# The beginning of a decoder layer: table load, first transfers, single k-tiles and the order of the first chunk

## The chip, the cores and the metric

The kernel runs on one core of a Trainium2 chip. The metric is the time of the program on the device in microseconds (us), the median of several executions; lower is better. A profiled execution gives the trace from which the rows below are read. Engines are named as the profile names them: PE (TensorE, matrix products), PEld (its weight loads), ACT (ScalarE), DVE (VectorE), POOL (GpSimd), SP (SyncE, which here only issues transfers). ACTq and SPq are the sequencers' transfer issues.

## What is computed

One layer of a hybrid decoder trunk on 256 tokens of width 2048. For the change only its beginning matters: the normalised memory `mem` times its key and value weights, before the input projection of `x`.

```python
def rms_norm(x, g):
    xf = x.astype(jnp.float32)
    y = xf * lax.rsqrt(jnp.mean(xf * xf, axis=-1, keepdims=True) + NORM_EPS)
    return (y * g.astype(jnp.float32)).astype(x.dtype)

def hybrid_layer(x, mem, ...):
    h = rms_norm(x, g_mix)
    proj = h @ w_in
    ...                                   # pooling, sparse attention
    mem_h = rms_norm(mem, g_mem)
    kv_m = mem_h @ w_mem_kv               # 256 x 2048 times 2048 x 1024
    k_m = rms_norm(kv_m[..., :XATTN_W].reshape(B, M, XATTN_HEADS, HEAD_DIM), xk_norm_g)
    v_m = kv_m[..., XATTN_W:].reshape(B, M, XATTN_HEADS, HEAD_DIM)
    ...                                   # cross attention, gates, output projection
    x = x + hierarchical_moe(rms_norm(x, g_ffn), ...)
    return x
```

## The kernel before

Products are made with split operands: each f32 operand is written as a high part (rounded, on ACT) and a low part (the rest, on DVE), and a product is three matmuls, high times high, high times low and low times high. `split_evac` (line 123) does that for weights: `wh` is a copy on ACT (line 124), `wl` a subtraction on DVE (line 125). `gain_split` (line 190) does it for the transposed activations, one k-tile of 128 x 256 at a time, with the norm's gain (a column of the constants `cs`) folded in: the high part on ACT (line 195), the low part on DVE (line 196).

The memory comes in four quads `memq[0..3]` of four k-tiles (128 x 4 x 256, 512 KB each), the weights of one chunk of 512 columns in four tiles `rawt` of four k-tiles (1 MB each, four buffers). `feeder` (line 229) loads `rawt` tile by tile on SP's queue (`load`, line 198) and, behind each load, what is listed under `after_load`: the next quad of the memory for the first chunk, quads of `x` for the second. Each tile gives two pairs of k-tiles, `wh` and `wl`, in three buffers each. `fetch(n)` draws from the feeder until `n` pairs are ready ahead.

`chunk` (line 259) runs over eight pairs of k-tiles: it fetches up to three pairs ahead, makes the 12 matmuls of a pair (line 274: two token tiles, two k-tiles, three products), then calls `pump`, which advances the background work by one step. During the first chunk, called km, the background is `mem_steps`: for quads 1, 2 and 3 the squares of the quad (`rm.square`, lines 169 and 172 on ACT, the sum with `tensor_add` on POOL, line 173) and its `gain_split`, then an empty step, then `rm.done` (line 175): matmuls that sum the squares (lines 179 and 184), the copy `row` (line 180) and the chain for 1/sqrt (`rsqrt`, lines 147 to 157, 14 operations of 128 x 2 on DVE). The result `rmr` scales the products when they are copied out of PSUM (`km_evac`, line 353). The second chunk, vm, has the same operand and, in the background, the same work on `x` for `hT`, the operand of the third.

The order of the instructions on an engine is set by a scheduler that goes by a timeline of its own. `keep_in_program_order` ties an instruction behind the one that was traced before it on its engine. `pin` (line 110) does so as long as the list `inorder` isn't empty; `load` and `warm` always do. Before the change the list is emptied ahead of the first chunk, behind the first two pairs (line 359).

At the start, 12 matmuls on a zeroed tile `z` run on PE (`warm`, line 301).

Of the kernel before, what the change touches and what calls it, by code (L numbers as in the profile page):

```python
# [15 lines left out]
AF = mybir.ActivationFunctionType  # L16
# [28 lines left out]
C_GMEM = 420  # L45
# [8 lines left out]
def layer_kernel(tc, x, xT, memT, pos, cst, band, gains, bgate, wmem, wxq, widx, wkqvp, wpg, wgb, wo, wr, we, out):  # L54
    nc = tc.nc
    V = nc.vector
    A = nc.scalar
# [50 lines left out]
    inorder = [True]  # L108

    def pin(i):  # L110
        if inorder:
            tc.keep_in_program_order(i)
# [10 lines left out]
    def split_evac(ps, hi, lo):  # L123
        pin(A.activation(hi, ps, AF.Copy))  # L124
        pin(V.tensor_sub(lo, ps, hi))  # L125
# [10 lines left out]
    ones32 = cp.tile([P, 32], F32, name="ones32")  # L136
    V.memset(ones32, 1.0)
    cs = cp.tile([P, C_N], F32, name="cs")
    nc.scalar.dma_start(cs, cst)
    big = cp.tile([P, NT, D], F32, tag="big", name="xin")  # L140
    
    xin = big.rearrange("p t d -> p (t d)").rearrange("p (k s) -> p k s", s=S)
# [16 lines left out]
    class RowRstd:  # L159
# [6 lines left out]
        def square(self, q, src):  # L166
            if q == 0:
                self.acc = scr.tile([P, 4, S], F32, tag="sqa", name="sqa", bufs=1)
                A.activation(self.acc, src, AF.Square)
            else:  # L170
                sq = scr.tile([P, 4, S], F32, tag="sq", name="sqT", bufs=1)
                A.activation(sq, src, AF.Square)
                nc.gpsimd.tensor_add(self.acc, self.acc, sq)

        def done(self):
# [14 lines left out]
    def gain_split(src, gc, dst, q, ks=slice(0, 4)):  # L190

        for k in range(ks.start, ks.stop):
            g = cs[:, gc + 4 * q + k : gc + 4 * q + k + 1]
            hi, lo = dst.q[q][:, 0, k], dst.q[q][:, 1, k]
            pin(A.activation(hi, src[:, k], AF.Copy, scale=g))
            pin(V.scalar_tensor_tensor(lo, src[:, k], g, hi, op0=ALU.mult, op1=ALU.subtract))

    def load(dst, src):
        tc.keep_in_program_order(nc.sync.dma_start(dst, src))
# [3 lines left out]
    def pump(n=1):  # L203
        for _ in range(n):
            while bg:
                try:
                    next(bg[0])
                    break
                except StopIteration:
                    bg.popleft()  # L210

    def drain():
        while bg:
            pump()
# [14 lines left out]
    def feeder():  # L229

        for ci, (src, n) in enumerate(plan):
            for i in range(4):
                rt = raw.tile([P, 4, n], F32, tag="raw", name="rawt")
                if ci == 0 and i == 0:
                    load(rt[:, 0:2], src[:, 0:2, :])
                    load(memq[0][:, 2:4], memT[0][:, 2:4])
                    load(rt[:, 2:4], src[:, 2:4, :])
                else:
                    load(rt, src[:, 4 * i : 4 * i + 4, :])
                for f in after_load.get((ci, i), ()):  # L240
                    f()
                for j in range(2):
                    s = rt[:, 2 * j : 2 * j + 2, :]
                    wh = spl.tile([P, 2, n], F32R, tag="wh", name="wh")
                    wl = spl.tile([P, 2, n], F32R, tag="wl", name="wl")
                    split_evac(s, wh, wl)
                    yield wh, wl

    feed = feeder()
    fed = deque()  # L250

    def fetch(n):
        while len(fed) < n:
            w = next(feed, None)
            if w is None:
                return
            fed.append(w)
# [45 lines left out]
    z = scr.tile([P, 512], BF16, tag="zero", name="zero", bufs=1)  # L303
# [5 lines left out]
    mT = Quads(lambda i: mtp.tile([P, 2, 4, S], F32R, name="memT%d" % i))  # L309
# [4 lines left out]
    def c4(name):  # L314
        return crp.tile([P, 4, S], F32, tag="c4", name=name, bufs=4)
# [11 lines left out]
        return done  # L327

    memq = [c4("memq") for _ in range(4)]
    load(memq[0][:, 0:2], memT[0][:, 0:2])  # L330

    def at(key, fn, *args):
        after_load.setdefault(key, []).append(lambda: fn(*args))
# [6 lines left out]
    def mem_steps():  # L340
        for q in range(1, 4):
            rm.square(q, memq[q])
            gain_split(memq[q], C_GMEM, mT, q)
            yield
        yield
        yield from rm.done()
# [5 lines left out]
            km.append(tok(c4("km")))  # L352
        A.activation(km[0][:, t], ac, AF.Copy, scale=rm.r[:, t : t + 1])

    gain_split(memq[0], C_GMEM, mT, 0, slice(0, 2))
    fetch(1)
    gain_split(memq[0], C_GMEM, mT, 0, slice(2, 4))
    fetch(2)
    inorder.clear()
    rm.square(0, memq[0])  # L360
    bg.append(mem_steps())
    chunk(512, [(KD, mT, km_evac)], name="km")
    drain()
    km = km[0]

# [170 lines left out]
    bias = [ap.tile([P, (t + 1) * P], F32, name="bias%d" % t) for t in range(NT)]  # L536
# [785 lines left out]
```

## Time and profile before

| | before |
|---|---|
| median of 3 runs | 1180.93 us (1178.69 to 1185.09) |
| the profiled execution | 1179.43 us |
| its span, first to last instruction | 1177.6 us |
| PE busy | 1146.5 us, 97% of the span |
| DVE busy | 576.6 us, 49% |
| ACT busy | 424.4 us, 36% |
| POOL busy | 30.3 us, 3% |
| granted clock of PE, mean | 0.992 |

The profiled execution is 1.8 us longer than its span; that is what lies around the first and the last instruction. A row of a timeline has the start in us, the time in us, the engine, the line, the operation, what it writes and reads, how many instructions are merged in it, and in brackets how long the engine was idle ahead of it and what ended that. A merged row's time runs from the start of its first instruction to the end of its last. Ends of matmuls are modelled, so the distance of their starts says more than their length.

### The profile page before, as it was taken

What the parts mean: (1) busy time and instruction counts of PE and PEld (TensorE: products, weight loads), DVE (VectorE), ACT (ScalarE), POOL (GpSimd) and SP (SyncE); (2) the same over time, 40 slices, a digit from 0 to 9 for tenths busy, and PEclk for the clock granted to TensorE, in tenths of its full rate; (3) what the DMA queues carried; (4) which work ended last, traced back from release to release, by engine and by line L of the source; (5) the groups of instructions that cost most, each with busy time, mean ns of one, the idle gap of its engine ahead of it and who ended that gap; (6) DMA issues with size and microseconds to landing.
All of it is one profiled execution on the core that took longest, in us unless ns stands there. A gap on an engine that the chain in (4) does not pass through costs nothing.

```text
span 1177.6 us, 14726 instructions
## 1 busy us (share of the span) xinstructions
PE 1146.5 (97%) x5863; PEld 790.0 (67%) x5863; DVE 576.6 (49%) x946; ACT 424.4 (36%) x664; POOL 30.3 (3%) x33
## 2 busy tenths in 40 slices
PE   8999999999999999999999999999999999999986
PEld 5788887888878888888888776454534544363423
DVE  7877468956546456456555445231413332151202
ACT  7665574445644444444444443111101201020100
POOL 4200000000000000000000000000000000000000
PEclk9999999999999999999999999989999999999998
DMA  9546554555645555555698759989999999999995
GB/s 382 203 129 229 184 178 146 178 186 179 225 157 200 208 193 205 201 194 208 219 346 359 281 212 339 423 340 426 425 427 426 425 427 427 425 425 427 425 427 218
DMA packets 50190, 342.45 MB, mean 291 GB/s; under 512 B 5696, under 2 KB 6336, under 8 KB 10432
## 3 DMA queue, kind: packets, MB, share of 16 engines
q1 hardware_dynamic: 46800, 331.93, 72.6%
q0 software_dynamic: 1728, 7.15, 1.7%
q10 hardware_dynamic: 1584, 2.34, 0.6%
q8 instruction: 48, 0.79, 0.3%
q14 instruction: 30, 0.25, 0.1%
HBM read 337.20 MB, written 4.19 MB: 290 GB/s over the span
## 4 chain that ended last, share of the span: by engine, by line


## 5 line engine op out<-in xcount | busy, mean ns | idle before, releaser
L274 PE MATMUL acc<-wh,hT 128*128 128x512 f32 (+1 forms) x1280 | 396.0, 388 | 0.0
L125 DVE TENSOR_TENSOR wl<-rawt,wh 128x1024 fp32r<-128x1024 f32 (+1 forms) x240 | 289.8, 1210 | 210.0 <-ACT wh L124 209.0
L124 ACT ACTIVATE wh<-rawt 128x1024 fp32r<-128x1024 f32 (+1 forms) x240 | 250.8, 1048 | 297.8 <-PE acc L274 290.9
L274 PEld LDWEIGHTS acc<-wh,hT 128*128 128x128 f32 x1280 | 238.3, 188 | 46.6 <-issue 0.3
L274 PE MATMUL acc<-wl,hT 128*128 128x512 f32 (+1 forms) x640 | 249.2, 390 | 0.0
L274 PEld LDWEIGHTS acc<-wl,hT 128*128 128x128 f32 x640 | 120.2, 188 | 24.0 <-DVE isc L585 0.3
L833 PE MATMUL gu<-we,xg 128*64 128x512 f32 x464 | 103.8, 595 | 1.8 <-DMA we<-in_we_dram 1.8
L274 PE MATMUL acc<-wh,mgT 128*128 128x512 f32 x256 | 81.7, 397 | 0.0
L833 PEld LDWEIGHTS gu<-we,xg 128*64 128x64 f32 x464 | 32.2, 137 | 64.8 <-issue 55.3
L958 ACT ACTIVATE xs<-x 128x256 fp32r<-128x256 f32 x61 | 24.8, 415 | 97.7 <-PE sm L833 86.9
L1169 DVE TENSOR_TENSOR x<-x,sm 128x512 f32<-128x512 f32 (+1 forms) x66 | 41.3, 668 | 38.0 <-PE sm L833 38.0
L1159 ACT ACTIVATE ob<-dn 128x512 fp32r<-128x512 f32 (+1 forms) x33 | 19.3, 585 | 104.1 <-PE dn L833 97.9
L274 PEld LDWEIGHTS acc<-wh,mgT 128*128 128x128 f32 x256 | 47.9, 188 | 11.4 <-issue 0.4
L1160 DVE TENSOR_TENSOR ob<-dn,ob 128x512 fp32r<-128x512 f32 (+1 forms) x33 | 22.3, 675 | 66.0 <-ACT ob L1159 65.9
L274 PE MATMUL acc<-wl,mgT 128*128 128x512 f32 x128 | 51.2, 400 | 0.0
L1146 DVE SCALAR_TENSOR_TENSOR sgm<-sgm,fac,gu 128x512 f32<-128x512 f32 x8 | 6.0, 748 | 90.8 <-PE gu L833 90.8
L1138 ACT ACTIVATE sgm<-gu,fac 128x512 f32<-128x512 f32 x8 | 5.5, 687 | 115.9 <-PE gu L833 69.2
L833 PE MATMUL dn<-we,aT 128*64 128x256 f32 x384 | 45.6, 384 | 1.4 <-ACT aT L1153 1.4
L833 PE MATMUL gu<-wm,xg 128*64 128x512 f32 x184 | 43.5, 594 | 1.3 <-DMA wm<-in_we_dram 1.3
L833 PE MATMUL gu<-wh,xg 128*64 128x512 f32 x200 | 44.7, 595 | 0.0
L274 PE MATMUL acc<-wh,memT 128*128 128x512 f32 x128 | 42.4, 408 | 1.3 <-ACT wh L124 1.3
L833 PE MATMUL gu<-wr,xg 128*64 128x512 f32 x176 | 41.7, 594 | 0.5 <-DMA wr<-in_we_dram 0.5
(338 smaller groups left out, 1196.4 us busy)
## 6 DMA issues: line engine op xcount, KB each, us to landing
we<-in_we_dram SPq DMA_DIRECT2D x82, 1024.0 KB, 19.4
rawt<-in_wgb_dram SPq DMA_DIRECT2D x64, 1024.0 KB, 4.8
wh<-in_we_dram SPq DMA_DIRECT2D x37, 1024.0 KB, 19.2
wr<-in_we_dram SPq DMA_DIRECT2D x36, 1024.0 KB, 19.5
wm<-in_we_dram SPq DMA_DIRECT2D x36, 1024.0 KB, 19.5
rawt<-in_wkqvp_dram SPq DMA_DIRECT2D x24, 1024.0 KB, 4.9
rawt<-in_wo_dram SPq DMA_DIRECT2D x16, 1024.0 KB, 4.9
rawt<-in_wmem_dram SPq DMA_DIRECT2D x7, 1024.0 KB, 8.3
```

What stands on the lines that cost most here:

```text
L124: pin(A.activation(hi, ps, AF.Copy))
L125: pin(V.tensor_sub(lo, ps, hi))
L274: m = mm(o, a[:, c], w[:, kk], start=st, stop=sp)
L833: i = mm(*a, **k)
L958: pin(A.activation(xs[:, 0], x2[:, :, c], AF.Copy))
L1138: A.activation(sg, ag, AF.Sigmoid, scale=r2s)
L1146: V.scalar_tensor_tensor(sg, sg, c1s, au, op0=ALU.mult, op1=ALU.mult)
L1159: A.activation(ob[:, 0], ad, AF.Copy)
L1160: V.tensor_sub(ob[:, 1], ad, ob[:, 0])
L1169: V.tensor_add(ys, ys, ps)
```

## The change

The constants `cs` and the first quad of the memory are issued on ACT's queue, the quad in pieces (k-tile 0, then `cs`, k-tile 1, k-tiles 2 and 3), while SP's queue begins with the weights, now in pieces of one, one and two k-tiles. A one-element copy on ACT stands behind these issues, ahead of the first gain. The first two pairs are split k-tile by k-tile: gain of a k-tile, then its weights, from inside the feeder. `rm.square` is pinned too, and the list `inorder` is emptied behind the first chunk, not ahead of it.

```diff
     cs = cp.tile([P, C_N], F32, name="cs")
-    nc.scalar.dma_start(cs, cst)
...
             if q == 0:
                 self.acc = scr.tile([P, 4, S], F32, tag="sqa", name="sqa", bufs=1)
-                A.activation(self.acc, src, AF.Square)
+                pin(A.activation(self.acc, src, AF.Square))
             else:
                 sq = scr.tile([P, 4, S], F32, tag="sq", name="sqT", bufs=1)
-                A.activation(sq, src, AF.Square)
+                pin(A.activation(sq, src, AF.Square))
                 nc.gpsimd.tensor_add(self.acc, self.acc, sq)
...
                 if ci == 0 and i == 0:
-                    load(rt[:, 0:2], src[:, 0:2, :])
-                    load(memq[0][:, 2:4], memT[0][:, 2:4])
+                    load(rt[:, 0:1], src[:, 0:1, :])
+                    load(rt[:, 1:2], src[:, 1:2, :])
                     load(rt[:, 2:4], src[:, 2:4, :])
...
-                    split_evac(s, wh, wl)
+                    if ci == i == 0:
+
+                        for kk in range(2):
+                            k = 2 * j + kk
+                            gain_split(memq[0], C_GMEM, mT, 0, slice(k, k + 1))
+                            split_evac(s[:, kk], wh[:, kk], wl[:, kk])
+                    else:
+                        split_evac(s, wh, wl)
                     yield wh, wl
...
     memq = [c4("memq") for _ in range(4)]
-    load(memq[0][:, 0:2], memT[0][:, 0:2])
+
+    def load2(dst, src):
+        tc.keep_in_program_order(nc.scalar.dma_start(dst, src))
+
+    load2(memq[0][:, 0:1], memT[0][:, 0:1])
+    load2(cs, cst)
+    load2(memq[0][:, 1:2], memT[0][:, 1:2])
+    load2(memq[0][:, 2:4], memT[0][:, 2:4])
+
+    tc.keep_in_program_order(A.activation(ones32[:, 0:1], z[:, 0:1], AF.Copy, bias=1.0))
...
-    gain_split(memq[0], C_GMEM, mT, 0, slice(0, 2))
-    fetch(1)
-    gain_split(memq[0], C_GMEM, mT, 0, slice(2, 4))
     fetch(2)
-    inorder.clear()
     rm.square(0, memq[0])
     bg.append(mem_steps())
     chunk(512, [(KD, mT, km_evac)], name="km")
+    inorder.clear()
     drain()
```

## Rows read from the trace of the kernel before

**Rows 1.** Windows: start:end, length, busy time and instructions per engine, PEclk, DMA.

```profile
0.00:61.00 61.00, 55.37 (x229) 39.64 (x230) 49.36 (x76) 42.79 (x70) 20.43 (x14) 0.97 0.73 284
61.00:200.00 139.00, 139.00 (x665) 115.70 (x664) 96.50 (x220) 82.59 (x176) 1.10 (x2) 1.00 0.53 177
...
630.00:720.00 90.00, 89.64 (x442) 70.88 (x440) 41.26 (x44) 36.47 (x47) 0.50 (x2) 1.00 0.75 281
...
800.00:900.00 100.00, 98.38 (x598) 48.93 (x596) 30.80 (x60) 14.18 (x29) 0.00 (x0) 1.00 1.01 426
```

**Rows 2.** Timeline of PE, 0 to 61 us.

```profile
1.23 5.13 PE L301 MATMUL warm<-zero 128*128 128x512 bf16 x12 [1.23 <-DVE zero L304]
7.68 0.73 PE L274 MATMUL acc<-wh,memT 128*128 128x512 f32 x2 [1.32 <-ACT wh L124]
...
15.48 0.86 PE L274 MATMUL acc<-wh,memT 128*128 128x512 f32 x3
...
18.70 0.86 PE L274 MATMUL acc<-wh,memT 128*128 128x512 f32 x3
...
27.51 0.40 PE L274 MATMUL acc<-wh,memT 128*128 128x512 f32 x1
...
34.32 0.63 PE L274 MATMUL acc<-wh,memT 128*128 128x512 f32 x2
...
49.90 0.64 PE L179 MATMUL ssT<-sqa,ones 128*32 128x256 f32 x8 [0.97 <-POOL sqa L173]
...
52.50 0.50 PE L274 MATMUL acc<-wl,memT 128*128 128x512 f32 x1 [1.30 <-DVE wl L125]
...
60.96 0.62 PE L274 MATMUL acc<-wh,hT 128*128 128x512 f32 x2
```

**Rows 3.** Timeline of DVE, 17 to 34 us.

```profile
17.50 3.81 DVE L196 SCALAR_TENSOR_TENSOR memT<-memq,cs,memT 128x256 fp32r<-128x256 f32 x4
21.23 2.35 DVE L125 TENSOR_TENSOR wl<-rawt,wh 128x1024 fp32r<-128x1024 f32 x2
...
27.25 2.34 DVE L125 TENSOR_TENSOR wl<-rawt,wh 128x1024 fp32r<-128x1024 f32 x2
...
30.98 1.66 DVE L196 SCALAR_TENSOR_TENSOR hT<-xin,cs,hT 128x256 fp32r<-128x256 f32 x4
...
33.95 0.16 DVE L187 TENSOR_SCALAR rmv<-ssv 128x2 f32<-128x2 f32 x1
```

**Rows 4.** Timeline of POOL, the first two sums of squares.

```profile
11.35 2.49 POOL L173 TENSOR_TENSOR sqa<-sqa,sqT 128x1024 f32<-128x1024 f32 x1 [10.04 <-ACT sqT L172]
15.79 4.05 POOL L173 TENSOR_TENSOR sqa<-sqa,sqT 128x1024 f32<-128x1024 f32 x1 [1.95 <-ACT sqT L172]
```

**Rows 5.** Timeline of ACT, 0 to 46 us.

```profile
0.73 0.41 ACTq L139 DMA_DIRECT2D cs<-in_cst_dram  x1
4.48 1.28 ACT L195 ACT_TABLE_LOAD   x1 [4.48 <-DMA memq<-in_memT_dram]
...
10.23 1.04 ACT L172 ACTIVATE sqT<-memq 128x1024 f32<-128x1024 f32 x1
11.17 1.69 ACT L195 ACTIVATE memT<-memq,cs 128x256 fp32r<-128x256 f32 x4
12.77 1.99 ACT L124 ACTIVATE wh<-rawt 128x1024 fp32r<-128x1024 f32 x2
...
45.16 1.27 ACT L353 ACTIVATE km<-acc,rmr 128x512 f32<-128x512 f32 x2 [3.07 <-DVE rmr L156]
```

**Rows 6.** Transfers: engine, count, size, us from issue to landing; issues at 0.7, 0.7, 3.2.

```profile
cs<-in_cst_dram ACTq DMA_DIRECT2D x1, 239.0 KB, 3.8
memq<-in_memT_dram SPq DMA_DIRECT2D x1, 256.0 KB, 3.7
...
rawt<-in_wmem_dram SPq DMA_DIRECT2D x1, 1024.0 KB, 8.3
```

**Rows 7.** Windows of 1 us: columns as in the first group.

```profile
10.00:11.00 1.00, 1.00 (x4) 0.81 (x3) 0.65 (x1) 1.00 (x2) 0.00 (x0) 0.50 0.97 406
```

**Rows 8.** Timeline of SP: the issue of the second weight tile.

```profile
3.24 0.44 SPq L199 DMA_DIRECT2D rawt<-in_wmem_dram  x1
```

## The prediction

> **What bounds the kernel now.** I read the windows of the whole span first, then the timelines of PE, ACT, DVE and POOL over the first 61 us. The windows [rows 1] say where a change at the beginning can be felt at all: in 0 to 61 us PE works 55.37 us, and in the next window it works 139.00 of 139.00; the five windows from 61 to 720 us hold 658.6 of 659 us. So nothing after 61 us absorbs or adds anything until 720 us: whatever the start is worth must be there when the matmuls on hT begin, at 60.96 in the execution before [rows 2], and from there it goes to the end one for one. Behind 720 us the expert weights fill the DMA engines (426 GB/s, share 1.01); their transfers start as PE frees buffers, so I let that stretch move along. The question is thus one number: when do the hT matmuls begin?
>
> The PE timeline [rows 2] gives the milestones. The 12 warm-up matmuls end at 6.36, the first real one begins at 7.68. I count in pairs of k-tiles, 12 matmuls each (2 token tiles x 2 k-tiles x 3 products). Pair 1 ends with the first matmul of the row at 15.48, pair 2 with the first of the row at 18.70, pair 5 with the row at 27.51, pair 7 (the last of chunk km) with the first of the row at 34.32: about 15.7, 18.9, 27.9 and 34.5. A matmul takes 0.233 from start to start at full clock (0.86 for three, less the 0.40 of the last, over two steps), so a pair costs 2.8.
>
> The DVE timeline [rows 3] shows the other bound. From 17.50 it works without a pause: four low parts of gain_split take 3.81, two wl 2.35, and so on. At 30.98 four low parts take only 1.66. The difference is POOL: its second add runs from 15.79 to 19.84 [rows 4], the low parts that begin at 17.50 end 1.5 behind that, and so I read that a low part is held until a running add ends. A wl subtraction is not held, but an add that meets two of them takes 4.05 in place of 2.49.
>
> **The table load.** Before, ACT loads its table from 4.48 to 5.76 [rows 5], because the load stands behind the wait for cs (issued 0.73, landed after 3.8: 4.53) and for memq (3.7) [rows 6]. After, ACT issues four transfers at 0.41 each (0.73 to about 2.4), then loads (1.28), done near 3.7, under the flight of the data. That removes 1.28 from ACT's start, if the data is there. It is not: cs is now second on its queue behind 128 KB, with the SP queue's weights beside it. Before, cs and memq, 495 KB, were there at 4.5; after, 128 + 239 KB on ACT's queue and as much of the weights are 734 KB, and at the 406 GB/s of a full window [rows 7] 239 KB more are 0.59: 5.1. If the 1 KB pieces of the single k-tile get a third of the engines instead of half, it is 862 KB, 5.4. If ACT's queue is served first, 4.4. I take 5.2: the first gain begins 0.55 earlier, not 1.28.
>
> The DMA engines are full in that row (share 0.97). The Trainium skill, "DMA: Bandwidth & Descriptors", section "Issuing engines are not separate DMA queues", says that transfers issued from several engines run on the same 16 DMA engines and interleave, and that spreading them saves issue time only. That speaks against this edit, and the full windows here agree: by it the edit is worth at most an issue time, where two independent paths would bring cs at 4.4 and the weights no later.
>
> **Single k-tiles.** A copy of 256 columns costs ACT 0.42 (four in 1.69), of 1024 columns 1.0 (two in 1.99) [rows 5]; 512 columns, which the trace lacks, lie between, in proportion 0.6. On DVE 0.42 and 1.17 give 0.67. So gain and wh of k-tile 0 end near 6.2 and the first matmul could begin there; the warm-ups hold PE to 6.36. PE starts 1.3 earlier than before. Cutting adds 2 x 0.6 - 1.0 = 0.2 to ACT and as much to DVE per pair; both wait for data there, so I put it at nothing; without that cover it is 0.4 for the two pairs. Pair 0 then ends near 10 and pair 1 near 12.9, against 15.7: a lead of 2.8, part of which is the half-clock stretch of before (granted clock 0.50 in 10:11 [rows 7]). The SP queue loses the two memq issues, which moves its later issues up by 0.9; as the engines are full, the landing of the next weights does not follow: the bytes ahead of it are the same.
>
> **Order kept.** This is the edit that decides. With inorder cleared only behind the chunk, every split, gain and square of km stays on ACT and DVE in the order of the code. That order is: wh of pair 2, square 1, gains q1, wh of pair 3, square 2, gains q2, wh 4, square 3, gains q3, wh 5, 6, 7. Before, the scheduler had square 1 (10.23) and gains q1 (11.17) ahead of wh 2 and 3 (12.77) [rows 5], likewise q2 ahead of 4 and 5, q3 ahead of 6 and 7. Two prices follow.
>
> First, wh 2 needs the second weight tile, which lands at 3.24 + 8.3 = 11.5 [rows 6, 8]. ACT, done with the first quad near 10.3, waits; behind it square 1 is queued, then the gains of q1. So wh 2 runs 11.5 to 12.5, square 1 ends at 13.5, the add runs to about 16.1 (before: 13.84), and the low parts of q1 end one by one from 16.5, in place of 14.3. Pair 2 can't use them sooner and ends near 19.0, before 18.9. The lead of 2.8 is used up here.
>
> Second, the low parts of q3 now stand ahead of wl 5, and all low parts are held by their adds. On DVE: low parts of q1 to 17.7, wl 3 to 18.9; add 2 begins behind those low parts and meets wl 3, 2.49 + 1.2, so to 21.3; low parts of q2 (1.66, the first with the add's end) to 22.9, wl 4 to 24.0; add 3 begins behind the low parts and meets wl 4, to 26.4; low parts of q3 to 28.1, wl 5 to 29.2, wl 6 30.4, wl 7 31.5. Before, wl 5 ended at 21.23 + 2.35 = 23.6 and wl 7 near 29.6 (27.25 + 2.34) [rows 3]. Pair 3 ends at 21.9; pair 4 between 25.0 and 26.7, as PE does the products without wl early or late; pair 5 between 30.1 and 31.8 (before 27.9), pair 7 between 36.8 and 38. Chunk km ends 2.3 to 3.5 later; I take 3.0.
>
> **Chunk vm.** Before, it loses 0.97 to POOL and 1.30 to wl [rows 2], as the chain for rmr, begun at 33.95 [rows 3], ends at 45.1 between other work, and the copy of km at 45.16, with 3.07 of waiting ACT [rows 5], holds the squares and gains behind it. After, wl 7 is queued behind the copy of row, and wl 8 behind the whole chain (each pinned instruction follows the one traced before it), so the chain runs undisturbed (15 operations of 0.16: 2.5) and km's copy is not late; the 2.27 may come back wholly or not at all, I take half, 1.1. The price: vm's first pair waits for the chain, from nothing (sums of row placed early among PE's matmuls) to about 5 (behind pair 7); I take 0.6. Sum: +3.0 - 1.1 + 0.6 = **+2.5** on the profiled execution's 1179.43, which lies 1.5 under the median; on the median 1180.93 it is **1183.4**. Its own range is +1 to +5: 1181.9 to 1185.9.
>
> **The rivals.**
> *The early start survives.* PE begins 1.3 earlier and does not stop, so the half-clock stretch goes: about eight matmuls at 0.43 in place of 0.233 cost 1.6. Together -2.9: 1178.0. The Trainium skill, "TensorE: Matmul & The Clock Gate", Part 1, has the clock halved behind idleness and full behind steady work; the row at 0.50 stands behind the gaps up to 7.68, which agrees. It needs gains of q1 that aren't late; for it speaks that the walk above rests on an order which I read from the code, against it the landing at 11.5. Chance 0.20.
> *The two ends cancel.* DVE's work to 61 us is nearly the same in both kernels, 49.36 [rows 1], and as it begins past 6 some 5 us of pauses are the reserve; if vm gives back all 2.27 and the chain hides, the hT matmuls begin within 0.7 of 60.96: 1181. This is also the case in which the change does not do what it says, as PE's end of vm is DVE's. Chance 0.20.
> *The chain stands in the way.* wl 8 waits on DVE behind the chain, the chain waits for the sums of row on PE, and these stand behind pair 6 or 7 in PE's order: before, the chain begins at 33.95, so that the second of them stands near the end of pair 7. If so, wl 8 comes near 41, PE waits some 4, and its clock may fall once more (1.6): +3.0 - 1.1 + 4 + 1.6 = +7.5, 1188.4. It decides from the point at which the sums stand behind pair 6. Chance 0.15.
> *The forecast* keeps 0.45.
>
> **How the numbers follow.** The time is the likeliest case's, 1183.4. The range takes in its own, the cancelling one, most of the surviving start and the lower half of the last: 1177.5 to 1188.0. A difference under 0.5%, 5.9 us, can't be told from no change here; the first three cases lie inside it with little left over. Faster by more would need twice the surviving start: 0.03. Slower by more is most of the last rival and a tail of the forecast: 0.13. The rest is 0.84.
>
> **What would show it.** In the trace of after: the table load before 4; the first gain near 5.2; the first real matmul at 6.4; ACT idle from about 10.3 to 11.5, with DMA as the releaser; the first add ending near 16; pair 2 ending near 19; PE waiting for wl behind pairs 3 and 4, near 22 to 24 and 26 to 29; km's copy near 38, without ACT waiting for rmr; hT matmuls near 63.5. I am wrong if ACT's order is not that of the code, if the second weight tile lands well before 11.5, or if the scheduler reorders work behind 61 us, which I left as it was.

## The result, and the profile after

The changed kernel takes 1187.93 us (median of 6 runs, 1186.82 to 1191.04) against 1179.99 us (6 runs, 1177.59 to 1185.09) of the kernel before: a ratio of 1.0076, 95% interval 1.0059 to 1.0093. This ratio and those below are the ones on record with their intervals; they are not quotients of the two medians (1.0067 here). The change is slower by 8 us where +2.5 was forecast. The profiled execution of after took 1188.25 us, its span 1186.5 (before 1179.43 and 1177.6).

The two windows that answer to [rows 1], columns as there:

```profile
0.00:61.00 61.00, 50.54 (x197) 34.66 (x198) 47.28 (x68) 39.81 (x62) 20.12 (x14) 0.94 0.72 267
61.00:200.00 139.00, 137.34 (x659) 114.80 (x658) 92.55 (x206) 82.87 (x178) 1.11 (x2) 1.00 0.52 175
```

PE lost 4.83 us of work to 61 us (55.37 before), and 1.66 us more behind it, in a window that had been full. The waits of PE over 1 us, from its timeline, and the first matmul on hT:

```profile
7.38 0.73 PE L280 MATMUL acc<-wh,memT 128*128 128x512 f32 x2 [1.59 <-ACT wh L124]
...
19.35 0.73 PE L280 MATMUL acc<-wh,memT 128*128 128x512 f32 x2 [1.23 <-DVE memT L195]
...
26.54 0.50 PE L280 MATMUL acc<-wl,memT 128*128 128x512 f32 x1 [1.80 <-DVE wl L125]
...
31.42 0.50 PE L280 MATMUL acc<-wl,memT 128*128 128x512 f32 x1 [1.05 <-DVE wl L125]
...
42.88 0.80 PE L280 MATMUL acc<-wl,memT 128*128 128x512 f32 x1 [2.36 <-DVE wl L125]
...
67.77 0.63 PE L280 MATMUL acc<-wh,hT 128*128 128x512 f32 x2
...
76.01 0.50 PE L280 MATMUL acc<-wl,hT 128*128 128x512 f32 x1 [1.67 <-DVE wl L125]
```

Before, PE waited at 7.68, 49.90 and 52.50 [rows 2]; the two in vm are gone, and all those above but the first have come. Counted in pairs of k-tiles as in the prediction (the end of a pair is the start of its last matmul plus 0.23):

| end of, us | before | after | lost in the stretch (minus: regained) |
|---|---|---|---|
| pair 2 | 18.93 | 21.31 | +2.4 |
| pair 7 (end of km) | 34.55 | 39.89 | +3.0 |
| first pair of vm | 37.34 | 46.65 | +4.0 |
| last pair of vm | 60.96 | 67.76 | -2.5 |
| 200 matmuls into hT | 99.69 | 108.97 | +2.5 |
| span | 1177.65 | 1186.47 | -0.5 |

**The start.** ACT's timeline, and the transfers of the first 14 us (size, us from issue to landing):

```profile
2.63 1.28 ACT L345 ACT_TABLE_LOAD   x1 [2.63 <-issue]
...
6.30 0.51 ACT L194 ACTIVATE memT<-memq,cs 128x256 fp32r<-128x256 f32 x1 [2.18 <-DMA cs<-in_cst_dram]
...
8.85 0.51 ACT L194 ACTIVATE memT<-memq,cs 128x256 fp32r<-128x256 f32 x1 [1.52 <-DMA memq<-in_memT_dram]
...
11.67 0.51 ACT L194 ACTIVATE memT<-memq,cs 128x256 fp32r<-128x256 f32 x1 [1.79 <-DMA memq<-in_memT_dram]
```

```profile
memq<-in_memT_dram ACTq DMA_DIRECT2D x1, 256.0 KB, 9.5
cs<-in_cst_dram ACTq DMA_DIRECT2D x1, 239.0 KB, 5.0
```

The table is loaded early, as meant, and then ACT waits for cs, for k-tile 1 and for k-tiles 2 and 3: three gaps of 2.18, 1.52 and 1.79. The last 256 KB of the quad, behind the other 495 KB of ACT's queue, land 9.5 us after their issue, at 11.65; before, the second half of the quad landed at 6.40. The second weight tile is issued at 4.78, not ahead of the 3.24 of before, and lands at 12.27 in place of 11.56. The two queues between 5 and 8 us (packets, MB, share of the engines' time; q1 is SP's, q10 ACT's):

```profile
q1 hardware_dynamic: 257, 0.93, 76.8%
q10 hardware_dynamic: 245, 0.30, 27.6%
```

They move nearly the same number of packets, but SP's carry 3.6 KB on the mean and ACT's 1.2 KB, so that ACT's queue gets a quarter of the bytes.

**The chain.** DVE's timeline at the end of km and the start of vm, and what POOL does there:

```profile
35.48 0.14 DVE L186 TENSOR_SCALAR rmv<-ssv 128x2 f32<-128x2 f32 x1
...
36.26 2.37 DVE L153 TENSOR_TENSOR rmt<-rmt,rmv 128x2 f32<-128x2 f32 x1
...
39.34 0.49 DVE L195 SCALAR_TENSOR_TENSOR hT<-xin,cs,hT 128x256 fp32r<-128x256 f32 x1
...
41.53 0.16 DVE L155 TENSOR_TENSOR rmr<-rmr,rmt 128x2 f32<-128x2 f32 x1
41.61 3.49 DVE L125 TENSOR_TENSOR wl<-rawt,wh 128x1024 fp32r<-128x1024 f32 x3
```

```profile
36.20 2.41 POOL L172 TENSOR_TENSOR sqa<-sqa,sqT 128x1024 f32<-128x1024 f32 x1 [7.44 <-ACT sqT L171]
```

The chain begins behind the sums of row on PE, which stand two matmuls into pair 6:

```profile
34.32 0.50 PE L183 MATMUL ssv<-cs,row 128*128 128x1 f32 x4
```

Three low parts of weights (the row at 41.61, merged) stand behind the chain for 1/sqrt. The chain takes 6.2 us: one operation of 128 x 2 takes 2.37 us, held while POOL adds squares of x, and four low parts of x (the first at 39.34) slip in between its steps. The same 15 steps for x, later and nearly undisturbed, take 2.9:

```profile
70.36 0.16 DVE L186 TENSOR_SCALAR rxv<-ssv 128x2 f32<-128x2 f32 x1 [3.63 <-PE ssv L183]
...
73.14 0.16 DVE L155 TENSOR_TENSOR rxr<-rxr,rxt 128x2 f32<-128x2 f32 x1
```

So of the 6.2 us, 2.9 are the steps, 2.2 the hold and 1.1 the four low parts. The trace of before already had a chain that takes 11.2 us, with such holds in it (its step at 39.63 takes 2.43 in place of 0.16); the prediction read only its two ends. PE waits 2.36 for the first low part behind the chain, and then runs at the lower of its two levels (1.2 of 2.4 GHz):

```profile
43.00:44.00 1.00, 1.00 (x3) 0.81 (x4) 1.00 (x2) 1.00 (x2) 0.00 (x0) 0.50 0.00 0
44.00:45.00 1.00, 1.00 (x4) 0.81 (x3) 1.00 (x1) 1.00 (x3) 0.98 (x1) 0.50 0.35 41
```

The pair takes 6.76 in place of 2.79, so the clock adds 6.76 - 2.79 - 2.36 = 1.6.

**The third chunk.** ACT squares the keys (`sq`, eight of them) around the copies of vm and makes `wh` for the third chunk behind both. Before, from hT at 60.96:

```profile
58.89 0.29 ACT L447 ACTIVATE sq<-km 128x128 bf16<-128x128 f32 x1
...
63.09 1.99 ACT L124 ACTIVATE wh<-rawt 128x1024 fp32r<-128x1024 f32 x2
```

After, from hT at 67.77, with the low part that PE then waits for:

```profile
66.80 0.69 ACT L332 ACTIVATE vm<-acc,rmr 128x512 f32<-128x512 f32 x1 [1.32 <-PE acc L280]
...
68.55 0.30 ACT L459 ACTIVATE sq<-km 128x128 bf16<-128x128 f32 x1
...
71.89 3.09 ACT L124 ACTIVATE wh<-rawt 128x1024 fp32r<-128x1024 f32 x3
```

```profile
74.72 1.23 DVE L125 TENSOR_TENSOR wl<-rawt,wh 128x1024 fp32r<-128x1024 f32 x1
```

Before, `wh` begins 2.1 us behind the start of hT, after 4.1, and its low part then stands behind two chains on DVE, those of x and km.

### The profile page after: what moved, and what is told of

It is laid out like the page before. It is cut to its first block, busy times and chain, and to the rows that moved or that the text cites. A ratio compares the mean times of both kernels' runs of the same rounds, so it can differ in the third digit from the quotient of the medians.

```text
span 1186.5 us, 14734 instructions
## 1 busy us (share of the span) xinstructions
PE 1149.1 (97%) x5863; PEld 790.3 (67%) x5863; DVE 578.4 (49%) x948; ACT 425.9 (36%) x667; POOL 30.0 (3%) x33
## 4 chain that ended last, share of the span: by engine, by line
## 5 line engine op out<-in xcount | busy, mean ns | idle before, releaser
L125 DVE TENSOR_TENSOR wl<-rawt,wh 128x1024 fp32r<-128x1024 f32 (+2 forms) x242 | 290.2, 1202 | 213.0 <-ACT wh L124 212.0
L124 ACT ACTIVATE wh<-rawt 128x1024 fp32r<-128x1024 f32 (+2 forms) x242 | 251.4, 1041 | 300.9 <-PE acc L280 295.6
```

## The experiments

All ratios are to the kernel before on the same chip, with 95% intervals; its medians there lie between 1178.12 and 1180.20 us. The trace is of one run of each kernel. "Start of hT" is the start of the first matmul on hT in the profiled execution (60.96 before, 67.77 after).

### One part of the change alone

**The order alone**: the kernel before with pinned squares, the list emptied behind the chunk.

```diff
...
-    inorder.clear()
     rm.square(0, memq[0])
     bg.append(mem_steps())
     chunk(512, [(KD, mT, km_evac)], name="km")
+    inorder.clear()
```

> The kernel before with the kept order alone: squares pinned, the list emptied behind the chunk; table, queues and whole splits as before. If the kept order carries the loss: first matmul at 7.7 as before, pair 2 ends near 19, pair 5 at 30 to 32, pair 8 waits for the chain and ends 6 to 9 us later than 37.3, hT begins at 64 to 67, the time is 5 to 8 us over the kernel before (1185 to 1188). If the queue carries it: within 2 us of before.

1184.67 us, 1.0054 (1.0037 to 1.0070); start of hT 64.33. Behind the start PE's waits over 1 us are three of those of after:

```profile
23.62 0.50 PE L274 MATMUL acc<-wl,memT 128*128 128x512 f32 x1 [1.81 <-DVE wl L125]
39.97 0.50 PE L274 MATMUL acc<-wl,memT 128*128 128x512 f32 x1 [2.16 <-DVE wl L125]
...
72.55 0.50 PE L274 MATMUL acc<-wl,hT 128*128 128x512 f32 x1 [1.64 <-DVE wl L125]
```

So the order makes a wait for a low part of km's weights, the wait for the chain and the wait in hT, without any change of the start.

**ACT's queue alone**, once in the change's manner with two halves of the quad, once as one transfer with rows of 4 KB.

```diff
-    nc.scalar.dma_start(cs, cst)
...
-                    load(memq[0][:, 2:4], memT[0][:, 2:4])
...
-    load(memq[0][:, 0:2], memT[0][:, 0:2])
+    tc.keep_in_program_order(nc.scalar.dma_start(memq[0][:, 0:2], memT[0][:, 0:2]))
+    tc.keep_in_program_order(nc.scalar.dma_start(cs, cst))
+    tc.keep_in_program_order(nc.scalar.dma_start(memq[0][:, 2:4], memT[0][:, 2:4]))
```

> The kernel before with the queues alone: the first quad in two halves of 256 KB on ACT's queue, cs between them, SP's queue begins with the weights; table load, splits and order as before. If ACT's queue gets the smaller share while SP's descriptors are larger, the second half lands at 9 to 11 in place of 6.4, pair 1 ends 2 to 3 us later than 15.7, hT begins at 62 to 64 and the time is 2 to 6 us over the kernel before. If two queues share the engines evenly, the second half lands near 7 and the time is within 1 us of before.

> The kernel before with the first quad on ACT's queue in one transfer of 4 KB rows, behind cs; nothing else changed (table load at the first gain, whole splits, free order). In two pieces of 2 KB rows ahead of and behind cs it cost 7.7 us and the first matmul came at 11.5. If short rows and the late cs made that: cs lands near 5.2, the quad near 7.5, the first matmul comes at 10 to 10.5, and the time is 2 to 5 us over the kernel before. If any use of ACT's queue upsets the scheduler's order as much, it stays 6 to 8 us over.

Halves: 1188.92 us, 1.0065 (1.0043 to 1.0088). Whole: 1187.07 us, 1.0075 (1.0058 to 1.0092). Without the early table load the load itself stands behind the later operand. In the kernel with one transfer:

```profile
8.01 1.28 ACT L194 ACT_TABLE_LOAD   x1 [8.01 <-DMA memq<-in_memT_dram]
...
11.21 1.22 PE L272 MATMUL acc<-wh,memT 128*128 128x512 f32 x2 [5.05 <-ACT wh L124]
```

Its start of hT is 67.15. The quad landed at 7.94, as the second expectation had it, yet the time stayed: the queue costs about as much by itself as the whole change does, and large rows don't cure it. A part of that is the late table load, which the change doesn't have; the run with the order undone, below, is free of it.

**The table load alone**, and with it the single splits, transfers and order as before.

```diff
+    tc.keep_in_program_order(A.activation(ones32[:, 0:1], z[:, 0:1], AF.Copy, bias=1.0))
```

> The kernel before with the one-element copy alone, behind the first issue on ACT's queue: the table is loaded early, transfers, splits and order as before. The first gain begins with the landing of cs and memq near 4.6 in place of 5.77, the first matmul waits for the warm-ups until 6.4 (7.7 before). If the start is worth what it gains, hT begins 0 to 1.3 us earlier and the time is 0 to 1.5 us under the kernel before; if a shifted start is lost in DVE's work, it is within 0.5; if the scheduler's order alone is upset by any shift (rival), it is 2 to 4 us over.

> Early table load and single k-tiles on ACT and DVE, order free, but the transfers of the kernel before (pieces of two k-tiles, 2 and 4 KB in a row). With single pieces on SP's queue the second weight tile landed at 12.8 in place of 11.56. If the short rows cost that: it lands at 11.5 to 11.7 again, pair 2 ends about 1 earlier than with single pieces (20.1), and the time is 0 to 2 us under that run's 1180.8. If the number of transfers costs it, half of the 1.2 stays.

Table: 1178.85 us, 0.9994 (0.9982 to 1.0007). With single splits: 1179.89 us, 0.9991 (0.9979 to 1.0003). Neither differs from the kernel before. In the second PE begins 1.1 earlier (6.58) and ends pair 1 at 12.54, 3.2 ahead; then it waits twice for the second weight tile's parts, its clock falls, and pair 2 ends at 20.21, 1.3 behind the kernel before. The tile had landed at 11.50; the second wait is long because the low parts of q1, the first of them held 2.33 by POOL's add, stand ahead of `wl` on DVE:

```profile
13.79 0.73 PE L280 MATMUL acc<-wh,memT 128*128 128x512 f32 x2 [1.08 <-ACT wh L124]
16.34 0.50 PE L280 MATMUL acc<-wl,memT 128*128 128x512 f32 x1 [1.81 <-DVE wl L125]
```

```profile
18.00:19.00 1.00, 1.00 (x4) 0.80 (x3) 1.00 (x1) 0.18 (x1) 1.00 (x1) 0.50 0.97 410
```

### One part undone

The list emptied ahead of the chunk (the order of before), the quad in single pieces on SP's queue, and both.

```diff
                     load(rt[:, 0:1], src[:, 0:1, :])
+                    load(memq[0][:, 1:2], memT[0][:, 1:2])
                     load(rt[:, 1:2], src[:, 1:2, :])
+                    load(memq[0][:, 2:4], memT[0][:, 2:4])
...
-    load2(memq[0][:, 0:1], memT[0][:, 0:1])
     load2(cs, cst)
-    load2(memq[0][:, 1:2], memT[0][:, 1:2])
-    load2(memq[0][:, 2:4], memT[0][:, 2:4])
+    load(memq[0][:, 0:1], memT[0][:, 0:1])
```

> The changed kernel without its last part: the list inorder is emptied ahead of chunk km again; table load, ACT's queue and single k-tiles stay. If the kept order carries the loss, the pairs behind pair 2 no longer wait for wl behind the low parts of q2 and q3, and wl of pair 8 is not queued behind the chain: pair 5 ends near 30, hT begins at 61 to 63.5, the time is 0 to 2.5 us over the kernel before (1180 to 1182.5). If the late first quad on ACT's queue carries it, most stays: hT begins at 66 or later, 5 to 8 us over.

> The changed kernel with the pieces of the first quad back on SP's queue, each ahead of its weights; cs alone on ACT's queue; single k-tiles, table load and kept order stay. If shares of the two queues made the first quad late (8.8 and 11.7 for k-tiles 1 and 2 to 3): these land by 5.8 and 7, the first gain begins near 4.6, the second pair's gains near 7, and pair 2 ends near 19 to 20 in place of 21.3, 2 us earlier than in the changed kernel. If the kept order carries the rest, the time stays 5 to 7 us over the kernel before (1185 to 1187); if the queue carries it all, it is at or under the kernel before.

> Early table load and single k-tiles without the other two parts: the pieces of the first quad on SP's queue, each ahead of its weights, cs alone on ACT's queue, the list emptied ahead of chunk km. If ACT's queue made the loss of the run without the kept order (hT at 64.2, 61.0 before): first matmul near 6, pair 1 ends near 13, pair 2 at 18 to 19, hT begins at 60 to 61.5 and the time is from 2 us under to 1 us over the kernel before. If the single k-tiles or the scheduler's new order made it: hT near 63 to 64, 3 to 6 us over.

Order undone: 1187.38 us, 1.0079 (1.0062 to 1.0095), start of hT 64.24. Queue undone: 1187.06 us, 1.0079 (1.0062 to 1.0095), start of hT 65.70. Both undone: 1180.83 us, 1.0011 (1.0002 to 1.0021), start of hT 62.41. So the loss has two sufficient causes. In the time, neither is seen by taking back the other; only both together bring it near the kernel before. With the queue undone pair 2 still ended at 21.19, a miss: the second weight tile now landed at 12.91, and the gains of q1 stood behind its `wh`.

One run had cs and then the whole quad in one transfer on ACT's queue, with the rest of the change.

> The changed kernel with ACT's queue cut to two transfers: cs first, then the whole first quad in one (4 KB in a row per partition in place of 1, 1 and 2 KB). It tells what sets the share of a queue. If the engines take turns by rows of a transfer, larger rows get a larger share: the whole quad, 512 KB, lands at 7 to 9, earlier than the 11.7 of its last piece in the changed kernel. If ACT's queue is served after SP's whatever the rows, it lands at 11 or later again.

1186.94 us (one run; the kernel before 1179.2 there). The quad landed at 7.53, as the first reading had it, and pair 2 ended at 19.14, near the forecast's 19.0. The late pieces thus cost the start 2.2 us. Of these 2.1 are still there at the start of hT (65.72 in place of 67.77) and 1.3 at the end of the span (1185.16 in place of 1186.47); what a single run of each shows of the end can be scatter.

### Where the tie ends

The list emptied between the last gains of km and the sums (`rm.done`), so that the low parts of vm's weights are not tied behind the chain: in the changed kernel, in the one with SP's queue, and in the order alone.

```diff
         yield
+        inorder.clear()
         yield from rm.done()
```

> The changed kernel with one line: the list is emptied ahead of the sums of the squares (background step 5), so that wl of pairs 7 and 8 is not tied behind the copy of row and the chain for 1/sqrt. If that tie costs 2.4 of waiting and 1.6 of half clock at pair 8: pairs 0 to 7 end as in the changed kernel (39.9), pair 8 at 42.7 in place of 46.7, and 1 to 4 us of it are left in the time (1184 to 1187). If the wait is DVE's load in any order, pair 8 stays near 46 and so does the time, 1188.

> The changed kernel with two parts undone: the pieces of the first quad on SP's queue, and the list emptied ahead of the sums of squares. What is left of the kept order is gains before splits in chunk km. If that alone still costs: pairs 2 and 5 end near 21 and 31 to 32, pair 8 follows pair 7 by 2.8 without waiting, hT begins near 62 to 64, the time is 2 to 5 us over the kernel before. If queue and tie were all of the loss: within 1 us of it.

> The kernel before with the kept order, but only up to the sums of squares, so that no wl is tied behind row or the chain. With the tie, the order alone cost 6.5 us (1184.7 against 1178.1). If the tie is most of it: pair 5 ends near 31 as with the tie, pair 8 follows pair 7 by 2.8, the time is 1 to 3 us over the kernel before. If gains ahead of splits are most of it: 4 to 6 us over.

In the changed kernel 1185.21 us, 1.0050 (1.0034 to 1.0067) for 1.0076; with SP's queue 1182.51 us, 1.0015 (1.0000 to 1.0030) for 1.0079; order alone 1183.63 us, 1.0036 (1.0022 to 1.0050) for 1.0054. In all three the first pair of vm takes 2.80, without a wait, where with the tie it takes 6.76, 5.42 and 5.23. By the ratios the tie costs 3.1, 7.5 and 2.1 us in the three. Only the second difference is clear of the intervals, so that the wait is shown and its price in the time is not well known. It may be more than they say: the three profiled runs each lost some 2 to 3 us by the end of pair 4 to a hold that is told under the next heading and that the runs they are compared with did not have. With the tie gone the queue shows: 1.0050 with ACT's, 1.0015 with SP's.

### The wait in the third chunk

The list filled again for the first pair of the third chunk, so that its weights go ahead of the eight squares of km. Before, three of these stand on ACT ahead of the copies of vm, two between and three behind; after, all stand behind.

```diff
-    chunk(512, [(KD, hT, evac(lambda t: xq[:, t], rx))], name="xq")
+    inorder.append(True)
+    chunk(512, [(KD, hT, evac(lambda t: xq[:, t], rx))], name="xq", step=lambda i: inorder.clear())
```

> The changed kernel with the first split of the third chunk (pair 18) in the order of the code, so that its wh stands ahead of the eight squares of km on ACT. If these squares and the chains behind them on DVE make the wait of 1.67 at 74.3 to 76.0, it goes or falls under 0.5, the third chunk's first 200 matmuls end 1.5 to 2.5 earlier against the start of hT, and the time is 1186 or less, against 1187.9. If the wait is made by the chain for x alone (it ends at 73.3), half of it stays.

1193.00 us, 1.0111 (1.0092 to 1.0131): slower, a miss. The first `wh` did go ahead, but its low part was now tied behind the chain of x, as vm's had been behind that of km, and PE's wait grew from 1.67 to 3.00. What makes the wait in the third chunk is thus read from the order in the traces; no run shows it by taking it away alone. The trace showed one thing more. Up to 60 us its engines run the same instructions in the same order as in the changed kernel, at first 0.02 us earlier; yet pair 4 ends at 32.67, not at 28.97. DVE and POOL of this kernel:

```profile
25.26 3.37 DVE L125 TENSOR_TENSOR wl<-rawt,wh 128x1024 fp32r<-128x1024 f32 x1
```

```profile
25.04 2.51 POOL L172 TENSOR_TENSOR sqa<-sqa,sqT 128x1024 f32<-128x1024 f32 x1 [1.17 <-ACT sqT L171]
```

And of the changed kernel:

```profile
25.27 1.22 DVE L125 TENSOR_TENSOR wl<-rawt,wh 128x1024 fp32r<-128x1024 f32 x1
```

```profile
25.05 3.71 POOL L172 TENSOR_TENSOR sqa<-sqa,sqT 128x1024 f32<-128x1024 f32 x1 [1.17 <-ACT sqT L171]
```

Either the one or the other waits: 3.71 is 2.49 of an add [rows 4] plus the 1.22 of wl, and the wl of 3.37 ends 1.1 behind the end of the add. Of the span's 5.3 us over after, 2.4 are there at the start of hT, from this, and 2.7 more in the third chunk. This prompted the last three kernels.

### Gains ahead of squares

In the background of km and of x each quad's gains are put ahead of its squares, in the kernel before and in that with the table load.

> The kernel before with one edit: in the background steps of both chunks the gains of a quad stand ahead of its squares, so that the low parts are made before POOL's add of that quad can run. If a low part is held until a running add ends, each group of four low parts takes 1.7 to 2 in place of 3.6 to 3.8, pair 2 ends 0 to 1 earlier than 18.9, pair 5 1 to 2 earlier than 27.7, and the time is 0 to 2.5 us under the kernel before. If low parts are slow for another reason (bandwidth shared with POOL in general), they take 3.6 still and nothing moves.

> Early table load alone and the gains ahead of the squares, transfers, whole splits and free order as before. With the table alone, pair 0 ended 2.3 earlier than before and pair 2 0.8 later, as PE waited 1.8 for q1 and its clock then fell. If the held low parts made that wait: it shrinks under 0.8, pair 2 ends near 17.5 to 18.5, and the time is 1 to 3.5 us under the kernel before. If the landing of the second weight tile (11.6) sets pair 2: it ends near 19 again, the time within 1 us.

1181.35 us, 1.0000 (0.9987 to 1.0013), and 1180.70 us, 1.0002 (0.9987 to 1.0017). The first group of low parts is no longer held (1.67 us for four), the later ones are. In the first of the two kernels pairs 2 and 5 end as before (18.92 and 27.74), and hT begins 0.7 earlier (60.27) in both; but all squares of km stand behind the copies of vm here too, and the third chunk gives it back in a wait of 1.67.

### The sums of squares on DVE

One line, in the changed kernel, in the kernel before, and in the one with table load and single splits.

```diff
-                nc.gpsimd.tensor_add(self.acc, self.acc, sq)
+                V.tensor_add(self.acc, self.acc, sq)
```

> The changed kernel with the sums of squares added on DVE in place of POOL, all else kept. Theory A (DVE and POOL hold each other off, and this is where chunk km lost its time): the three low parts that were held 2.6 us each become 0.47, a price of 6.4 us on DVE in km, against 3 additions of about 1.2 us there; the waits of PE for wl at 26.5 and 31.4 us (1.80 and 1.05) go or shrink below 0.5 each, pair 7 ends near 37 in place of 39.9, and the time falls by 3 to 4 us to about 1184.5, a ratio to the kernel before of 1.003 to 1.005. The wait of 2.36 us behind the chain at the start of vm stays, as the tie stays. Theory B (the order alone makes the loss, whoever adds): pair 7 ends within 0.7 of 39.9, and the ratio is 1.007 to 1.009.

> The kernel before with the sums of squares added on DVE in place of POOL. Theory A: no low part takes over 0.5 us; DVE loses six holds of about 2.2 us to 61 us and gains six additions of 1.2 us; PE's waits of 0.97 us for POOL near 49.9 and of 1.30 us for wl near 52.5 shrink, the hT matmuls begin 1 to 2.3 us earlier than 60.96, and the time is 0.9980 to 0.9992 of the kernel before. Theory B (the holds lie beside other work there): between 0.9995 and 1.001.

> Early table load, first four k-tiles split one by one, transfers and free order as before the change, and the sums of squares added on DVE. Theory A: the lead of the early start (pair 1 ends at 12.5 us) is lost at pair 2 because the low parts of the second quad are held by POOL's first add; without it they end by about 15 us, pair 2 ends near 16 to 17.5 us in place of 20.2, and the hT matmuls begin 2 to 3.5 us before 60.96: ratio 0.9965 to 0.9985. Theory B (the landing of the second weight tile at 11.5 us sets pair 2, whoever adds): pair 2 ends within 0.7 of 20.2 and the ratio is 0.9985 to 1.0005.

**In the kernel before** it takes 1175.28 us (12 runs, 1174.15 to 1176.51), 0.9964 (0.9953 to 0.9975): faster than both kernels, and by more than theory A gave it. The hT matmuls begin at 57.43. PE's only waits over 0.3 us to 700 us are the two of the first fence, and no low part is held (second fence, DVE: four in 1.67; 3.81 in [rows 3]):

```profile
7.80 0.73 PE L274 MATMUL acc<-wh,memT 128*128 128x512 f32 x2 [1.33 <-ACT wh L124]
9.06 0.50 PE L274 MATMUL acc<-wl,memT 128*128 128x512 f32 x1 [0.53 <-DVE wl L125]
```

```profile
18.23 1.67 DVE L196 SCALAR_TENSOR_TENSOR memT<-memq,cs,memT 128x256 fp32r<-128x256 f32 x4
```

It does so with a later start: POOL's transfer of 256 KB of gains, behind the last add at 49.78 before, is no longer behind anything there, goes out at 1.45, and the second weight tile lands at 13.4 in place of 11.56. That was not meant, and a version that holds it back was not run.

**In the changed kernel** 1187.46 us, 1.0069 (1.0042 to 1.0096): A is right in km and wrong at the chain. Here too POOL's transfer goes out early, and pair 1 ends 1.5 later (17.40). The holds are gone, the waits at 26.5 and 31.4 shrink to one of 0.79, and pair 7 ends at 37.56, 2.3 earlier. All of that is given back at the chain. The sums of row now stand two matmuls into pair 7 on PE, one pair later in its order than in after, so that the chain begins no earlier than there; it takes low parts of x and an addition in between, and ends at 41.5. PE waits 4.49 where A left the wait at 2.36:

```profile
34.80 0.50 PE L183 MATMUL ssv<-cs,row 128*128 128x1 f32 x4
```

```profile
41.42 3.49 DVE L125 TENSOR_TENSOR wl<-rawt,wh 128x1024 fp32r<-128x1024 f32 x3
```

```profile
42.69 0.79 PE L280 MATMUL acc<-wl,memT 128*128 128x512 f32 x1 [4.49 <-DVE wl L125]
```

The first pair of vm ends at 46.62, in after at 46.65. With the holds gone from both, the change costs 1187.46 - 1175.28 = 12 us.

**With the early start** 1176.20 us, 0.9970 (0.9957 to 0.9982), start of hT 57.47. Pair 2 ends at 18.66, 1.5 earlier than without the line but not at 16 to 17.5. Against the line alone the early start is worth nothing (57.47 and 57.43): the first matmul is 1.3 earlier, pair 1 is 2.3 earlier, pair 2 is not (18.66 and 18.63), as the second weight tile lands at 13.4 in both and PE waits for it:

```profile
14.81 0.73 PE L280 MATMUL acc<-wh,memT 128*128 128x512 f32 x2 [1.12 <-ACT wh L124]
16.23 0.50 PE L280 MATMUL acc<-wl,memT 128*128 128x512 f32 x1 [0.69 <-DVE wl L125]
```

## Why the prediction was wrong, point by point

The direction was right, and so was the order's part in it: kept alone, it costs some 6.5 us. That ACT's queue alone costs at least as much was not foreseen. The time came out at the number of the rival "the chain stands in the way", 1188.4, which had a chance of 0.15, but not by its working, which had the sums of row behind pair 6, a wait of 4, and nothing for pair 2 and the third chunk. That the numbers meet is luck.

- **The wait for the chain, 0.6.** This is the step that failed: it measured 4.0, 2.36 of waiting and 1.6 of half clock. I let the chain run undisturbed in 2.5. It takes 6.2, because only km's work is tied; the work on x is free and is placed between the chain's steps (1.1), and POOL's add of x holds one of them (2.2). The place of the sums was not at fault: they stand at 34.32, 0.47 behind the end of pair 5, earlier than the rival had them. With a chain of 2.9 from 35.48 the first low part behind it would be ready near 39.6, an estimate from these rows, and PE asked for it at 40.52. The kernels that end the tie at the sums have no such wait. In the changed kernel with the sums of squares on DVE no step is held, but the sums of row stand a pair later, and there the rival's case came true. The copy of km, forecast near 38, waited for the chain too and came at 41.73.
- **"Nothing behind 61 us", 0.** This failed too: +2.5. The full windows [rows 1] show that nothing was late there before, not that nothing can be. The prediction named work reordered behind 61 us as a sign of being wrong, and it came: the squares of km moved behind the copies of vm, ACT made the weights of the third chunk later, and their low part stood behind the chains of x and km, so that PE waited 1.67 up to 76.01. It comes with the order alone and with the swap. The traces fall into two groups by this: in six (before, the table load alone, the single splits with either size of rows, the sums on DVE without the new order, with and without the early start) three squares stand ahead of the copies and 200 matmuls of hT take 38.73 or 38.74; in all others all eight stand behind them, and it is 39.9 to 41.3, and 43.9 with the list filled again.
- **cs at 5.2.** It landed at 6.21, outside the bounds of 4.4 and 5.4. (The lower bound was not worked out; the same sum gives 4.2.) I shared the stream by halves or thirds; ACT's short rows got a quarter of its bytes between 5 and 8 us. k-tiles 2 and 3 landed at 11.65, so the first quad was not done near 10.3 but near 13.6, and pair 1 ended at 15.9, not at 12.9. ACT's idle time thus stood ahead of gains, not ahead of wh 2 (landed 12.27).
- **Pair 2 at 19.0.** 21.31. The add ran 16.55 to 19.01 (forecast: to 16.1), and the low parts were held behind it, as argued; the late quad made 2.2 of it, as the run with the whole quad shows (pair 2 at 19.14), and most of that goes on to the start of hT.
- **Pairs 2 to 7, +2.9** (the forecast's +3.0 for km, less the 0.1 of pair 2). +3.0, with the waits of PE where they were forecast, behind pairs 3 and 4 (1.80 and 1.05). (Pair 5 of before ends at 27.74 by the prediction's own rule, not at 27.9.) The number hid a coin: had the add won at 25.05, it would have been +5.4.
- **vm recovers 1.1.** 2.5: both waits of [rows 2] in vm went, as could be, at the price of the chain.
- **Single splits and table load, at nothing.** Right: 0.9991 and 0.9994, and the lead was used up at pair 2, as forecast. The half-clock stretch of before [rows 7] also stayed (0.50 in 9 to 11), so the rival of the surviving start found no ground.

Of the sum, in the order of the table: +2.4 (forecast +0.1), +3.0 (+2.9), +4.0 (+0.6), -2.5 (-1.1), +2.5 (0), -0.5 (0): +8.8 of span, where +2.5 was forecast.

The order and the queue, each enough for a loss, don't add in the time (1.0079, 1.0079 and 1.0076 for both). In the traces they do add up to the start of hT: against the run with both undone (62.41) the queue brings 1.8, the order 3.3, both 5.4. Behind it, either tips the scheduler into the second group, whose 1.2 to 2.5 us are paid once. The rest lies behind the first 200 matmuls on hT, where one trace each of these four kernels scatters by 2.7 us, so that no cause can be named for it. What also stays open is what in the scheduler's own timeline tips it (ACT's queue and gains ahead of squares do, though pair 7 was no later with the latter), and how much of the scatter of the changed kernel, 1186.82 to 1191.04, is the coin between DVE and POOL.

## What to carry to other kernels

Before an order is pinned, list what is queued behind the slowest small chain on that engine, and end the pin ahead of the chain. An early start is worth what the next transfer and the next pair can use: price it at the second wait, not at the first. Ask of every pair of engines that read the same memory at the same time whether one waits for the other; here moving a sum from POOL to DVE, one line, brought 0.36%, more than any ordering.

## What the runs showed of the hardware

- **DVE and POOL exclude each other over whole instructions.** I had read that low parts are held and weight subtractions are not. Either can be: of the 14 cases in these traces in which a wl began 0.22 or 0.23 us behind an add, the add was stretched to about 3.7 in ten and the wl to about 3.4 in four, though the kernels run the same kind of work around it. In after and in the kernel with the list filled again it is the same instructions in the same order, and the outcome differs. The Trainium skill, "SBUF — State Buffer", section "SBUF: two separate sides", has it so: VectorE (with two inputs in SBUF) and GpSimd share a port pair by an exclusive lock, the first to start keeps it for its instruction and the other blocks. The rows agree on the exclusion. They don't show that the first recorded start wins, as POOL's stood first in all 14.
- **It holds small work too**: a 128 x 2 step of 0.16 us on DVE took 2.37 in after and 2.43 in before.
- **A queue's share of a full stream goes with its rows.** With both queues at work, after has 257 packets on SP's and 245 on ACT's, of 3.6 and 1.2 KB, and ACT's get 27.6% of the engines' time. With the quad in one transfer of 4 KB rows (ACT's queue alone, 4 to 7 us) the packets are again nearly as many on either, and the shares nearly even:

```profile
q1 hardware_dynamic: 195, 0.67, 55.3%
q10 hardware_dynamic: 186, 0.59, 48.4%
```

In the changed kernel the same 751 KB of ACT's queue had landed by 7.53 with the quad in one transfer, by 11.65 with it in pieces. The Trainium skill, "DMA: Bandwidth & Descriptors", section "Queues, rings and completion order", says that an engine takes turns between queues packet by packet, which fits.

- **Smaller pieces delay what follows.** With the first tiles in single k-tiles on SP's queue the second weight tile landed at 12.80 (early start, both other parts undone), with pieces of two at 11.50, the bytes ahead of it being the same. Whether the shorter rows or the larger number of transfers does it was not separated.
